# Single banks for all large products, the keys' columns as a pair, and branch sums loaded by the Pool queue, in a fused decoder layer

## The chip, the cores and the metric

The kernel runs on one core of a Trainium2 chip. The metric is the time of one execution on the device in microseconds (us). A core has five engines that run side by side and wait for each other on semaphores: TensorE (PE, matrix products out of SBUF into PSUM), VectorE (DVE), ScalarE (ACT), GpSimd (POOL) and SyncE (SP). DMA transfers are issued here from SP's queue and from POOL's. PSUM has eight banks of 128 x 512 fp32 values. Each engine takes its instructions strictly in the order written for it: an instruction that waits holds up all behind it on that engine or queue.

## The reference, cut to what matters

One layer of a hybrid decoder, for 512 prompt tokens and 8 x 4 sample tokens (T = 544 rows of x together), model width 2048:

```
u = x @ w_in            # split by columns: q_m k_m v_m o_m z_m (2048 each), q_a (2048),
                        # k_a v_a (256 each), z_a g_m g_a (2048 each), i f (4 each)
h_m = mLSTM(q_m, k_m, v_m, ig, log_sigmoid(f), state C, n, m)      # 4 heads of 512
h_a = sliding window attention(q_a, k_a, v_a, 128 wide, ALiBi, sinks)   # 32 heads of 64, 4 kv heads
br_m = headnorm(h_m) * sigmoid(o_m) * silu(z_m);   br_a = h_a * silu(z_a)
y   = sigmoid(g_m) * (br_m @ w_proj_m) + sigmoid(g_a) * (br_a @ w_proj_a)
out = layernorm(alpha * x + y @ w_out)
# also put out: new C, n, m, and key/value buffers of the window:
k_buf_sample = concat(state_attn_k, k_a)[:, 4:];   v_buf_sample likewise
```

The sample rows attend to the window in `state_attn_k` and `state_attn_v`, and 124 of the 128 rows of each new buffer are copies of the old one. All is fp32.

## The kernel before, in words

**Products.** x is kept transposed, as 16 blocks k of [128, 544]. Every fp32 operand of a large product is split in a high part (an ACT cast to fp32r, `wh`, L196; for activations L236) and a low part (a DVE subtraction, `wl`, L197, or L237), and a product is hi·hi + hi·lo + lo·hi: three matmuls. There are two forms.

- `gemm` (L215): 128 output columns, 16 k x 3 x 2 halves of 272 rows = 96 matmuls of 128 x 272 (L205) into one "mm" tile of two PSUM banks. It is used for the columns of V and K of the attention, for all of w_proj_a, for columns 0 to 2 and 13 to 15 (of 16 blocks) of w_proj_m, and for w_out. `tick()` between k runs one step of the side work that is waiting.
- `paired` (L632): two blocks of 128 columns by a scheme of Strassen's kind: seven half products n = 0 to 6 of 24 matmuls each (`half_product`, L599 and L601), 168 in place of 192. It needs sums of the quarters of x (`s1`, `n2`, `n3`, `s4`; the list `XS`) and of the quarters of the weights, made in `prepare` (L572): t1 = b11 + b12, b11 = t1 + b22, b12 += b22, b21 += b11, by DVE adds (L579). Where a pair has `acc`, the last two go as accumulating DMA transfers of POOL's queue (L577). `gather` (L603) collects the products out of three single banks into two tiles. Weights for two products ahead are prepared at high priority.

Raw weights are loaded by SP into three buffers `raw` (b11, b12) and three `raw2` (b22, b21); there are two buffers each of `wh` and `wl`. A load waits on SP's queue until its buffer has been read for the last time.

**PSUM.** Four banks hold small results ("sm"). The other four are opened by `open_psum`: as two "mm" tiles of two banks for gemms, or as four "bank" tiles for pairs; it is called at each change of form.

**Stages.** 0 to 89 us: x comes in 16 loads of 128 x 512 and 4 of samples, is transposed on PE, four transposes to a PSUM tile, and split; two gemms for V, with the gates' products (L340) between their halves; two gemms for K. Beside them `x_sums` (L482) makes s1, n2 and n3 from the split parts, on DVE and in eight operations on POOL (L487, L491); `last_sum` makes s4 beside the first pair. After the K gemms, in SP's queue from 27 us, stand the copies of the old key and value states to their outputs (L541, L542, 992 KB each). 89 to about 1810 us: 72 pairs of columns of w_in, the first 35 with `acc`; the first ones are gates' and mLSTM columns as filling, then 16 pairs of q_a and z_a, each followed by a step of attention (`attentions`, L779; the keys of a kv head come back from scratch memory in `kv_head`, L679, L680, and are cast on ACT). To about 2120 us: 16 gemms of w_proj_a, with the prompt's mLSTM beside them. 2130 to 2320 us, the merge: three gemms of w_proj_m, five pairs, three gemms. Beside the first three `operand_sums` loads the branch br_m from scratch memory (L1406, on SP, four steps of two loads of 544 KB into two buffers) and makes the four sums that the pairs need; the pairs here have no `acc`. Then w_out and the layer norm, to the end.

**Order.** Instructions are put in each engine's order by a planner that works on the program with priorities: `tc.high_priority(offset=...)` moves what stands in it ahead by so much, and `tc.issue_after(x)` keeps DMA issues behind x. `spawn` and `tick` feed side work in small steps (each `yield` ends one).

Of the kernel before, what the change touches and what calls it, by code (L numbers as in the profile page):

```python
# [20 lines left out]
D = 2048  # L21
# [52 lines left out]
def _build(tc, nc, i, o, es):  # L74
# [111 lines left out]

    def load_half(wv, c0, half):
        raw = wr.tile([128, 8, 128], F32, tag="raw", name=nm("raw"))
        state["load"] = nc.sync.dma_start(raw[:], wv[:, half * 8:half * 8 + 8, c0:c0 + 128])
        return raw  # L190

    def split(raw, p=None, tags=("wh", "wl")):
# [3 lines left out]
        A.copy(wh[:], raw[:])  # L196
        V.tensor_tensor(out=wl[:], in0=raw[:], in1=r32(wh[:]), op=ALU.subtract)  # L197
        return wh, wl

    def products(ps, half, wh, wl, xh, xl, cols, every=8):  # L200
        for kk in range(8):
            k = half * 8 + kk
            for n, (a, b) in enumerate(((wh, xh), (wh, xl), (wl, xh))):
                for f, c, w in cols:
                    PE.matmul(ps[:, f, :w], a[:, kk], b(k, c, w),  # L205
                              start=(k == 0 and n == 0), stop=(k == 15 and n == 2))
# [4 lines left out]

    def mm():
        return psA["mm"].tile([128, 2, 512], F32, tag="mm", name=nm("mm"))

    def gemm(wv, c0, xh, xl, cols=EVEN, raws=(None, None), every=8, prio=0, before=None):  # L215
        ps = mm()
        for half in range(2):
# [3 lines left out]
            if prio:  # L221
                with tc.high_priority(offset=prio):
                    wh, wl = split(raw)
            else:
                wh, wl = split(raw)
# [3 lines left out]
    def pv(ps, r=ALL):  # L229
        return ps[r, :, :272]  # L230

    def psamp(ps, r=ALL):
        return ps[r, 1, 240:272]
# [32 lines left out]
    s1, n2, n3 = quad(act2, "s1"), quad(act2, "n2"), quad(act2, "n3")  # L266
# [3 lines left out]
    esG = ExitStack()  # L270
    t544 = pool(esG, "t544", 12)
    tx = pool(esG, "tx", 4)
# [4 lines left out]
    pxs = sm()  # L277
    raw0 = []
    xs_src = i["x_sample"].rearrange("b t d -> (b t) d")
    warm = sm()  # L280
    for _ in range(24):
        PE.transpose(warm[:, 0:128], ident, ident)
    for g in range(4):
        xt = []
        for t in range(4):
            x_ = t5(n=512)
            nc.sync.dma_start(x_[:], i["x_prompt"][0, t * 128:t * 128 + 128, g * 512:g * 512 + 512])
            xt.append(x_)
        xs = ev(512)
        nc.sync.dma_start(xs[:NS], xs_src[:, g * 512:g * 512 + 512])  # L290
        if g < 3:
# [1380 lines left out]
```

## Time and profile before

| | us |
|---|---|
| median of 3 runs | 2543.43 |
| lowest, highest | 2541.89, 2546.58 |
| profiled execution | 2540.61 |
| its span | 2538.8 |

| engine | busy us | share of the span |
|---|---|---|
| PE | 2506.1 | 99% |
| weight loads of PE | 2444.8 | 96% |
| DVE | 1774.0 | 70% |
| ACT | 1208.0 | 48% |
| POOL | 368.9 | 15% |

The granted clock of PE was 0.994 of full speed over the span. Rows of the profile read: start in us, duration in us, engine, line of the kernel, operation, what it writes, what it reads, and in square brackets how long the engine stood idle just before it and what released it. Names have their buffer numbers left out. An engine's busy time is no measure of what it costs; where PE stands idle, the releaser tells who was late.

### The profile page before, as it was taken

To read this page: it belongs to the slowest core of one execution; us is meant where nothing else is said; L and a number is where in the kernel's file an instruction comes from. 1 tells how busy PE (TensorE), PEld (TensorE's weight loads), DVE (VectorE), ACT (ScalarE), POOL (GpSimd) and SP (SyncE) were. 2 spreads that over 40 slices of the span, in tenths; PEclk is the share of its full clock that TensorE was granted. 3 is DMA by queue.
4 is the path that set the end of the run, shared out by engine and by line. 5 is a ranking of instruction groups with operands and counts; after the bars stand their busy time and mean duration, and the time that the engine had idled before them with its cause. 6 is when DMAs were issued, how large, how long until landed. Compare 5 with 4: busy or idle time off the path is not lost.

```text
span 2538.8 us, 48796 instructions
## 1 busy us (share of the span) xinstructions
PE 2506.1 (99%) x19874; PEld 2444.8 (96%) x19874; DVE 1774.0 (70%) x2595; ACT 1208.0 (48%) x1952; POOL 368.9 (15%) x339
## 2 busy tenths in 40 slices
PE   8999999999999999999999999999999999999997
PEld 7999999999999999999999999999999999999997
DVE  7867677777677777687777878777755654874236
ACT  4457676676676665433433434444633332433221
POOL 2111211211211211221111222211000000000002
PEclk9999999999999999999999999999999999999999
DMA  6576666666666654467576576575755556558432
GB/s 193 132 174 163 149 149 164 147 150 164 150 146 164 153 149 115 121 214 238 164 229 214 167 218 205 164 233 179 232 183 173 180 177 194 155 176 264 110 96 84
DMA packets 543026, 433.58 MB, mean 171 GB/s; under 512 B 44080, under 2 KB 449888, under 8 KB 542512
## 3 DMA queue, kind: packets, MB, share of 16 engines
q1 hardware_dynamic: 532720, 393.74, 51.7%
q0 software_dynamic: 10080, 36.70, 7.9%
q8 instruction: 156, 2.56, 0.4%
q14 instruction: 70, 0.57, 0.1%
HBM read 305.74 MB, written 90.04 MB: 156 GB/s over the span
## 4 chain that ended last, share of the span: by engine, by line
PE 91%; DVE 2%; DMA 1%; issue 1%; ACT 1%; SPq 0%; DVEq 0%; ACTq 0%
PE bank L599 41%; PE bank L601 20%; PE mm L205 16%; PE sm L1264 2%; PE sm L1084 1%; PE sm L1078 1%; PE sm L1296 1%; PE sm L705 1%; PE sm L1309 1%; PE sm L743 1%; PE sm L733 1%; PE sm L205 1%; DVE wl L197 1%; ACT wh L196 1%; DMA raw<-in_w_in 0%
## 5 line engine op out<-in xcount | busy, mean ns | idle before, releaser
L196 ACT CAST wh<-raw 128x1024 fp32r<-128x1024 f32 x619 | 648.2, 1047 | 876.5 <-PE bank L599 616.4
L197 DVE TENSOR_TENSOR wl<-raw,wh 128x1024 fp32r<-128x1024 f32 x619 | 763.9, 1235 | 300.7 <-ACT wh L196 266.0
L599 PE MATMUL bank<-xk,wh 128*128 128x272 f32 x2304 | 317.4, 288 | 0.0
L579 DVE TENSOR_TENSOR raw<-raw,raw 128x1024 f32<-128x1024 f32 x238 | 303.0, 1276 | 7.5 <-DMA raw<-in_w_in 3.3
L599 PEld LDWEIGHTS bank<-xk,wh 128*128 128x128 f32 x2304 | 299.8, 188 | 3.4 <-ACT wh L196 1.7
L618 POOL TENSOR_TENSOR ev<-p,ev 128x272 f32<-128x272 f32 x77 | 116.2, 1509 | 680.9 <-ACT ev L617 623.7
L601 PE MATMUL bank<-xk,wl 128*128 128x272 f32 x1152 | 171.0, 288 | 0.0
L599 PE MATMUL bank<-s4h,wh 128*128 128x272 f32 x616 | 159.5, 290 | 0.6
L599 PE MATMUL bank<-n3l,wh 128*128 128x272 f32 x616 | 159.5, 290 | 0.0
L599 PE MATMUL bank<-s1h,wh 128*128 128x272 f32 x616 | 159.3, 290 | 0.0
L599 PE MATMUL bank<-n3h,wh 128*128 128x272 f32 x616 | 159.1, 289 | 0.0
L599 PE MATMUL bank<-n2l,wh 128*128 128x272 f32 x616 | 158.6, 289 | 0.0
L599 PE MATMUL bank<-n2h,wh 128*128 128x272 f32 x616 | 158.6, 288 | 0.0
L599 PE MATMUL bank<-s1l,wh 128*128 128x272 f32 x616 | 158.6, 290 | 0.0
L599 PE MATMUL bank<-s4l,wh 128*128 128x272 f32 x616 | 158.3, 290 | 0.0
L601 PEld LDWEIGHTS bank<-xk,wl 128*128 128x128 f32 x1152 | 154.6, 188 | 0.0
L205 PE MATMUL mm<-bh,wl 128*128 128x272 f32 x704 | 148.3, 290 | 2.2 <-DVE wl L197 2.2
L599 PE MATMUL bank<-a11h,wh 128*128 128x272 f32 x576 | 149.0, 290 | 0.5 <-ACT wh L196 0.5
L599 PE MATMUL bank<-a11l,wh 128*128 128x272 f32 x576 | 148.8, 291 | 0.0
L205 PE MATMUL mm<-bh,wh 128*128 128x272 f32 x704 | 147.9, 291 | 0.6 <-DVE ev L628 0.6
L205 PE MATMUL mm<-bl,wh 128*128 128x272 f32 x704 | 147.9, 289 | 0.0
L599 PEld LDWEIGHTS bank<-s4h,wh 128*128 128x128 f32 x616 | 115.8, 188 | 2.1 <-ACT wh L196 1.7
(439 smaller groups left out, 5719.2 us busy)
## 6 DMA issues: line engine op xcount, KB each, us to landing
raw<-in_w_in SPq DMA_DIRECT2D x296, 512.0 KB
raw<-raw POOLq DMA_DIRECT2D x70, 512.0 KB, 5.0
C<-in_state_mlstm_C SPq DMA_DIRECT2D x32, 1024.0 KB
out<-C SPq DMA_DIRECT2D x64, 512.0 KB
raw<-in_w_proj_a SPq DMA_DIRECT2D x32, 512.0 KB
raw<-in_w_proj_m SPq DMA_DIRECT2D x32, 512.0 KB
raw<-in_w_out SPq DMA_DIRECT2D x32, 512.0 KB
d_sgm<-ev SPq DMA_DIRECT2D x16, 272.0 KB
```

The costliest lines, as they stand in the source:

```text
L196: A.copy(wh[:], raw[:])
L197: V.tensor_tensor(out=wl[:], in0=raw[:], in1=r32(wh[:]), op=ALU.subtract)
L205: PE.matmul(ps[:, f, :w], a[:, kk], b(k, c, w), start=(k == 0 and n == 0), stop=(k == 15 and n == 2))
L579: V.tensor_tensor(out=w[out][:], in0=w[a][:], in1=w[b][:], op=ALU.add)
L599: PE.matmul(ps, wh[:, k], x(p, k), start=(first and k == 0 and p == 0), stop=False, skip_group_check=True)
L601: state["end"] = PE.matmul(ps, wl[:, k], x(0, k), start=False, stop=(k == 7), skip_group_check=True)
L618: G.tensor_tensor(out=c22, in0=p1, in1=c11, op=ALU.subtract)
L705: PE.matmul(pp[:, c0 + w0:c0 + 256], qs[a][:, j * 128:j * 128 + 128], kx[:, k0:k0 + 256 - w0], start=(n == 0), stop=(n == 1))
L733: PE.transpose(pt[:, (m - m0_) * 128:(m - m0_) * 128 + 128], s_[:, b, 128:256] if own else s_[:, b + 1, 0:128], ident)
L743: PE.matmul(po[:, b * 128:b * 128 + n], VA[:, b], p_[:, 2 * b:2 * b + n // 128], start=(b == 0 and m == 0), stop=(b == 3 and m == 1), skip ...
L1078: PE.matmul(pC[c * 32:c * 32 + 32, :], qz[:, c], ct[:, c], start=(b == 0), stop=(b == NB - 1), tile_position=(0, c * 32))
L1264: PE.matmul(pp[:, 0:258], a[:, b * 128:b * 128 + 128], b_[:, b, f], start=(b == 0 and n == 0), stop=(b == 3 and n == 2))
```

## The change

- PSUM: `open_psum` is gone. Four single banks serve both forms. A gemm takes two of them, and what evacuates it is two operations of 272 in place of one of 544 (`halves`).
- Start: x comes in six loads of 128 x 4 x 256 or 512, the samples in two; the order of loads is x, weights, x, samples, x, weights, and so on; 20 instead of 24 warm-up transposes. The raw sums of x are made on DVE from the transposes' PSUM tiles and the parts just split (`s1r`, `n2r`, `n3r`); POOL has none of them. `x_sums` then finishes n2, splits the three, and after V makes s4 in place. Constants and biases are loaded after x. The priority in this stage is 500 where it was 150.
- Keys: the two gemms of K become one pair, the first of the work list, with `acc`; there are 73 pairs in that list now. `attn_values` and `attn_keys` begin some ticks later, and the gates' chain is cut in more steps.
- The copies of the states, 2 x 992 KB, and of the new rows to them, move from the end of the K gemms to the opening of `attentions`. The negation of the sinks moves there too.
- Merge: the five pairs of w_proj_m have `acc`; `operand_sums` has eight steps of one k pair, each with one load of [128, 2, 544] by POOL's queue, and the sums and splits are 272 wide, 64 operations of DVE for 32. The priority of the six gemms' splits is 400 where it was 150.

The core of the diff:

```diff
-    esP, psA = es.enter_context(ExitStack()), {}
-
-    def open_psum(pairs):
-
-        esP.close()
-        psA["mm"] = pool(esP, "psP" if pairs else "psA", 4 if pairs else 2, PSUM)
-
-    open_psum(False)
+    psA = pool(es, "psA", 4, PSUM)
...
+    def bank():
+        return psA.tile([128, 512], F32, tag="bank", name=nm("bank"))
+
     def mm():
-        return psA["mm"].tile([128, 2, 512], F32, tag="mm", name=nm("mm"))
...
+        return [bank(), bank()]
...
+    for _ in range(20):
+        PE.transpose(warm[:, 0:128], ident, ident)
+    raw0, xt, xs = [], [], []
+    for c0, n in ((0, 256), (256, 256), (512, 512), (1024, 512), (1536, 256), (1792, 256)):
+        t_ = xr.tile([128, 4, n], F32, tag=f"x{n}", name=nm("xr"))
+        xdma = nc.sync.dma_start(t_[:], xp_src[:, :, c0:c0 + n])
+        xt += [t_[:, :, c:c + 128] for c in range(0, n, 128)]
+        if c0 == 0:
+            raw0.append(load_half(win, VA_, 0))
...
             else:
-                hilo(pt[:], xk2[0][g - 2][:, q, 0:SEQ], xk2[1][g - 2][:, q, 0:SEQ])
...
+                hilo(pt[:], xk2[0][k // 4 - 2][:, k % 4, 0:SEQ], xk2[1][k // 4 - 2][:, k % 4, 0:SEQ])
+                c = (slice(None), k - 8, slice(0, SEQ - HT))
+                V.tensor_tensor(out=s1r[c], in0=pt[:, HT:SEQ], in1=s1r[c], op=ALU.subtract)
...
+                for ch in (g - 1, g):
+                    ks_ = two_k(ch)
+                    V.tensor_tensor(out=s1r[:, ks_], in0=r32(a21[0][:, ks_]), in1=r32(a21[1][:, ks_]), op=ALU.add)
...
+        if g == 3:
+            for ch in range(4):
+                ks_ = two_k(ch)
+                V.tensor_tensor(out=n2r[:, ks_], in0=r32(a11[0][:, ks_]), in1=r32(a11[1][:, ks_]), op=ALU.add)
+                V.scalar_tensor_tensor(n3r[:, ks_], n2r[:, ks_], -1.0, s1r[:, ks_], op0=ALU.mult, op1=ALU.subtract)
...
     def x_sums():
-
         for ch in range(4):
...
-            G.tensor_tensor(out=r21[:], in0=r32(a21[0][:, ks_]), in1=r32(a21[1][:, ks_]), op=ALU.add)
...
-            G.tensor_tensor(out=r11[:], in0=r32(a11[0][:, ks_]), in1=r32(a11[1][:, ks_]), op=ALU.add)
...
     def ahead_of_sums():
-        return tc.high_priority(offset=150)
+        return tc.high_priority(offset=500)
...
-    for kk in range(2):
-        ps = gemm(win, KA + kk * 128, xh, xl, every=4, prio=150)
-        kt = ev()
-        with ahead_of_sums():
-            A.copy(two(kt[:]), pv(ps))
-            attn_keys(kk, kt)
-    drain()
-    for src, dst in ((d_ks, kb_s), (d_vr[SEQ:T], vb_s)):
-        nc.sync.dma_start(dst[:, 124:128].rearrange("b t k d -> b t (k d)"), src.rearrange("(b t) c -> b t c", t=NTS))
-    nc.sync.dma_start(kb_s[:, 0:124], i["state_attn_k"][:, NTS:128])
-    nc.sync.dma_start(vb_s[:, 0:124], i["state_attn_v"][:, NTS:128])
...
     def attentions():
         while gates_ in live:
             yield
-        for _ in last:
-            pass
         esG.close()
+        with tc.issue_after(state["gates_end"].ins):
+            V.tensor_scalar(nsinkb[:], sinkb[:], -1.0, None, op0=ALU.mult)
+        with tc.issue_after(state["load"].ins):
+            for src, dst in ((d_ks, kb_s), (d_vr[SEQ:T], vb_s)):
+                nc.sync.dma_start(dst[:, 124:128].rearrange("b t k d -> b t (k d)"),
+                                  src.rearrange("(b t) c -> b t c", t=NTS))
+            nc.sync.dma_start(kb_s[:, 0:124], i["state_attn_k"][:, NTS:128])
+            nc.sync.dma_start(vb_s[:, 0:124], i["state_attn_v"][:, NTS:128])
...
+    def end_keys(o1, o2):
+        for kk, o_ in enumerate((o1, o2)):
+            spawn(attn_keys(kk, o_))
...
-    work = [fill.pop(0) for _ in range(3)]
+    work = [pair(KA, KA + 128, end_keys)] + [fill.pop(0) for _ in range(3)]
...
-        for ch in range(4):
-            two_ = []
-            for k in (2 * ch, 2 * ch + 8):
-                t_ = tx.tile([128, 2, T], F32, tag="tx", name=nm("tx"))
-                nc.sync.dma_start(t_[:], src[k:k + 2].rearrange("k p t -> p k t"))
-                two_ += [t_[:, :, 0:HT], t_[:, :, HT:T]]
-            r11, r21, r12, r22 = two_
-            ks_ = slice(ch * 2, ch * 2 + 2)
+        for k in range(8):
+            t_ = tx.tile([128, 2, T], F32, tag="tx", name=nm("tx"))
+            G.dma_start(out=t_[:], in_=src[k:k + 9:8].rearrange("k p t -> p k t"))
+            r11, r21, r12, r22 = (t_[:, a, c:c + HT] for a in range(2) for c in (0, HT))
...
-        sg = merge(pv(gemm(wm, ct * 128, bmh, bml, every=4, prio=150)))
+        sg = merge([p_[:, :HT] for p_ in gemm(wm, ct * 128, bmh, bml, every=4, prio=AHEAD)])
...
-    paired([dict(wv=wm, x=XM, cA=ct * 128, cB=ct * 128 + 128, scale=1.0, end=end_merge(ct)) for ct in range(3, 13, 2)])
+    paired([dict(wv=wm, x=XM, cA=ct * 128, cB=ct * 128 + 128, scale=1.0, acc=True, end=end_merge(ct)) for ct in range(3, 13, 2)])
```

More of the change, by code (lines that the diff above doesn't have):

```diff
@@ L195, in split @@
         wl = p.tile([128, 8, 128], F32R, tag=tags[1], name=nm("wl"))
-        A.copy(wh[:], raw[:])
-        V.tensor_tensor(out=wl[:], in0=raw[:], in1=r32(wh[:]), op=ALU.subtract)
+        n = 8 // parts
+        for k in range(0, 8, n):
+            A.copy(wh[:, k:k + n], raw[:, k:k + n])
+            V.tensor_tensor(out=wl[:, k:k + n], in0=raw[:, k:k + n], in1=r32(wh[:, k:k + n]), op=ALU.subtract)
         return wh, wl
@@ L1384, in _build @@
         ps = gemm(wa_, ct * 128, bah, bal, every=2)
[L1385 removed]
+        for p_, s_ in halves(ps, sg):
+            V.tensor_tensor(out=s_, in0=p_, in1=s_, op=ALU.mult)
         nc.sync.dma_start(d_t[ct], sg[:])
```

227 lines of the change are left out of this document (125 added, 102 removed).

## The prediction

> **What bounds the kernel now.** I read the page first, then the busy time in stretches of 20 us, then TensorE's own timeline at each stretch that is not full, and from there the engine named as releaser.
>
> ```profile
> span 2538.8 us, 48796 instructions
> PE 2506.1 (99%) x19874; PEld 2444.8 (96%) x19874; DVE 1774.0 (70%) x2595; ACT 1208.0 (48%) x1952; POOL 368.9 (15%) x339
> PE 91%; DVE 2%; DMA 1%; issue 1%; ACT 1%; SPq 0%; DVEq 0%; ACTq 0%
> ```
>
> PE (TensorE) is busy 99% of the span and carries 91% of the chain that ended last. So there are two ways to win: fewer matmuls, or closing the few holes. The stretches say where the holes are (columns: stretch, its length, busy PE, weight load, DVE, ACT, POOL each with its count, granted clock, DMA share, GB/s):
>
> ```profile
> 0.00:20.00 20.00, 13.51 (x74) 11.88 (x75) 6.57 (x14) 6.47 (x14) 2.96 (x7) 0.83 0.88 255
> 20.00:40.00 20.00, 19.67 (x158) 18.55 (x157) 16.43 (x30) 10.92 (x28) 6.45 (x5) 1.00 0.68 201
> 40.00:60.00 20.00, 16.33 (x117) 15.83 (x117) 19.74 (x27) 10.51 (x19) 8.17 (x8) 0.91 0.54 146
> 120.00:140.00 20.00, 19.41 (x151) 18.64 (x151) 11.87 (x20) 8.16 (x13) 2.72 (x3) 1.00 0.68 152
> 140.00:160.00 20.00, 20.00 (x162) 20.00 (x161) 12.61 (x15) 10.27 (x14) 3.17 (x3) 1.00 0.86 214
> 2160.00:2180.00 20.00, 16.90 (x121) 16.49 (x120) 17.21 (x22) 6.90 (x10) 0.00 (x0) 0.91 0.59 193
> 2260.00:2280.00 20.00, 19.03 (x151) 18.62 (x150) 15.77 (x19) 8.20 (x10) 1.44 (x1) 1.00 0.46 137
> 2280.00:2300.00 20.00, 19.38 (x155) 19.19 (x154) 14.63 (x21) 9.34 (x13) 0.00 (x0) 1.00 0.98 313
> ```
>
> A full stretch holds 162 matmuls, 0.123 us each. Counting what is missing against 162 at 0.125 us: 40 to 60 us lacks 45 (5.6 us), 120 to 140 lacks 11 (1.4), 2160 to 2180 lacks 41 (5.1), the two around 2280 lack 11 and 7 (2.3). The first 20 us are filling. In 40 to 60 us DVE (VectorE) is busy 19.74 of 20: that stretch is DVE's, not PE's. The holes themselves:
>
> ```profile
> 43.01 1.11 PE L460 MATMUL sm<-cc,ev 128*128 128x128 f32 x4 [2.39 <-ACT ev L530]
> 44.81 0.43 PE L205 MATMUL mm<-a21l,wh 128*128 128x272 f32 x1
> 45.04 0.43 PE L205 MATMUL mm<-a11h,wl 128*128 128x272 f32 x1
> 46.77 0.29 PE L205 MATMUL mm<-a21h,wh 128*128 128x272 f32 x1
> 46.89 0.29 PE L205 MATMUL mm<-a11l,wh 128*128 128x272 f32 x1
> 57.11 0.52 PE L205 MATMUL mm<-xk,wl 128*128 128x272 f32 x2 [1.28 <-DVE wl L197]
> 89.06 0.33 PE L473 MATMUL sm<-cc,ev 128*128 128x128 f32 x1 [1.44 <-ACT ev L536]
> 89.26 0.37 PE L599 MATMUL bank<-a11h,wh 128*128 128x272 f32 x1
> 2165.09 0.52 PE L205 MATMUL mm<-bh,wl 128*128 128x272 f32 x2 [2.19 <-DVE wl L197]
> ```
>
> After the 2.39 us hole matmuls start 0.23 us apart (44.81, 45.04) until about 46.4, then 0.12 (46.77, 46.89): a hole of 2 us and more costs some 1.7 us again in slow matmuls. [...]
>
> **The change, part by part.**
>
> *Keys as a pair.* Two gemms of 96 matmuls become seven half products of 24: 168 instead of 192. 24 x 0.125 = 3.0 us off PE, in a place where nothing else can fill it. The pair needs the sums of x that the gemms did not, and so brings DVE's work on them forward by 26 us. That is the price, next.
>
> *Sums of x, start.* DVE's rows around the second V column block, whose low part PE waits for:
>
> ```profile
> 11.65 1.23 DVE L197 TENSOR_TENSOR wl<-raw,wh 128x1024 fp32r<-128x1024 f32 x1 [8.92 <-ACT wh L196]
> 28.87 0.68 DVE L237 TENSOR_TENSOR xk<-sm,xk 128x512 fp32r<-128x512 f32 x1
> 29.47 1.28 DVE L492 TENSOR_TENSOR tx<-tx,tx 128x544 f32<-128x544 f32 x1
> 41.68 1.22 DVE L197 TENSOR_TENSOR wl<-raw,wh 128x1024 fp32r<-128x1024 f32 x1
> 42.82 0.72 DVE L237 TENSOR_TENSOR s1l<-tx,s1h 128x544 fp32r<-128x544 f32 x1
> 43.45 0.72 DVE L237 TENSOR_TENSOR n3l<-tx,n3h 128x544 fp32r<-128x544 f32 x1
> 55.84 1.21 DVE L197 TENSOR_TENSOR wl<-raw,wh 128x1024 fp32r<-128x1024 f32 x1
> ```
>
> From start to start a 512-wide operation takes 0.60 us (28.87 to 29.47), a 1024-wide one 1.14, a 544-wide one 0.63; by width a 272-wide one comes to about 0.36 and a 240-wide one to 0.33 (estimates from these). In the changed kernel's instruction order DVE does ahead of that low part, that included: 3 of 1024, 22 of 544, 7 of 512, 8 of 272, 15 of 240 and 6 small ones of 0.2: 3.4 + 14.0 + 4.2 + 2.8 + 4.9 + 1.5 = 30.8 us. Before, the like count is 22.1 us, stretched by POOL at work beside it (the 1.28 for a 0.7 operation at 29.47) and by some 6 us of waiting for x. DVE began at 11.65 and was done at 42.9. After, POOL has no more sums, x comes in six larger loads, and DVE can start near 9.7 (the first weights' landing): 9.7 + 30.8 + about 2 of waiting = 42.5. So the first V hole barely moves: DVE trades idle time and contention for eight more microseconds of its own work. The wait at 43.01 on the copy of V vanishes (the transposes now come some ticks later), but the low part takes its place 0.4 us earlier.
>
> The second low part stood at 55.84 to 57.05. After, 4.2 us of last sums and low parts of x, 0.3 of gates, 5.1 of s4, 1.1 of a pair's add and its own 1.1 follow 43.3: 55.7. PE: 48 matmuls more, 61.7; the low parts of s4 and of the first pair are queued behind, 4 x 0.63 + 1.14, and I add 1.8 us for them: the first half product at 63.5. The pair takes 168 x 0.125 = 21.0 and the transposes of keys 0.5: 85.0 against 89.26. **−4.2 us** for start and keys, 3.0 of it the matmuls. Bounds: −2 if DVE waits longer for x than 2 us, −11 if none of the holes at 43, 57 and 89 nor the filling is left (9.2 us of holes and slow clock, less what the filling must keep, with the 3.0). I take −4.2 because DVE's own count bounds it. The gates' chain is cut into more steps (about 11 more turns); nobody waits for it until the first attention, some 50 us later, so I cost it at nothing. The four warm-up transposes fewer stand before the first x has landed: nothing. Sinks' negation and constants later: nothing, same cover.
>
> *State copies and the keys' way to the attention.* The two 992 KB copies of the states move on SP's queue from 27 us to the opening of the attentions, right ahead of further weights and of the loads of keys from scratch memory.
>
> ```profile
> 27.10 0.79 SPq L541 DMA_DIRECT2D out<-in_state_attn_k  x1
> 34.94 5.30 SPq L189 DMA_DIRECT2D raw<-in_w_in  x1
> 127.32 1.42 SPq L679 DMA_DIRECT2D s<-d_ka  x2
> 127.61 1.05 ACT L196 CAST wh<-raw 128x1024 fp32r<-128x1024 f32 x1 [2.41 <-PE bank L599]
> 133.14 0.62 ACT L236 CAST k<-s 128x512 fp32r<-128x512 f32 x1 [4.48 <-DMA s<-d_ka]
> 133.97 1.04 ACT L196 CAST wh<-raw 128x1024 fp32r<-128x1024 f32 x1
> ```
>
> Before, the keys' load lands 5.8 us after issue (127.32 to 133.14), ACT stands 4.48 us, and the next weights' cast behind it (133.97) comes a little late: the 1.4 us of 120 to 140. After, the order on SP is: state copies, the next pair's weights, among them one whose buffer is freed only by the low part of the sixth product of the running pair, then the keys. ACT's cast of k stands between the weights' casts of products six and seven. Counted from the start of the fourth product (3 us each), PE bears a landing at +6.75; the buffer frees near +1 to +3, and with 1.8 us of issuing ahead and 5.8 of landing it comes at +8.6 to +10.6. That makes 1.9 to 3.9 us of hole, with slow matmuls 2.9 to 5.6, less the 1.4 there was: **+2.8 us**. Bounds: −1.4 if it is in time, +8 if the 2 MB of copies add to it the 5.3 us that the row at 34.94 shows for a load behind them. I take the middle, as the copies are issued some products earlier.
>
> *Merge.* Two things change by rows of the merge: four DVE adds a pair become two DMA accumulations on POOL's queue and two DVE adds; and the branch comes in eight loads of 544 KB on POOL's queue, one k pair each, instead of eight on SP's in four steps of two.
>
> ```profile
> 2136.36 0.43 SPq L1406 DMA_DIRECT2D tx<-d_brm  x1
> 2142.94 0.72 DVE L1410 TENSOR_TENSOR tx<-tx,tx 128x544 f32<-128x544 f32 x1 [2.51 <-DMA tx<-d_brm]
> 2155.79 9.65 SPq L189 DMA_DIRECT2D raw<-in_w_proj_m  x2
> 2157.52 0.72 DVE L1410 TENSOR_TENSOR tx<-tx,tx 128x544 f32<-128x544 f32 x1 [5.02 <-DMA tx<-d_brm]
> 2163.82 1.22 DVE L197 TENSOR_TENSOR wl<-raw,wh 128x1024 fp32r<-128x1024 f32 x1
> L577 POOL DMA_DIRECT2D raw<-raw x70: 848/860/1058, 79.9 to 896.6; - x70
> raw<-raw POOLq DMA_DIRECT2D x70, 512.0 KB, 5.0
> ```
>
> The 2.19 us hole comes from DVE: it stood 5.02 us for tx, then had six operations of a 544-wide step, an add and the previous block's merge ahead of the low part at 2163.82. Gone are 10 adds of 1.14 (11.4 us); 64 operations of 0.36 replace 32 of 0.63 (+2.9), and 16 merges in halves add 0.1 each (+1.4): some 7 us less on DVE. Stretches 2160 to 2180 and around 2280 lack 5.1 + 2.3 = 7.4 us together. What decides is L, the time from a load's issue to its landing, since DVE, in order, has a step's sums ahead of later low parts. Between freeing a buffer and using it again DVE has about 13 operations, 6.5 us, and the low parts behind have 1 to 1.5 us in hand: L up to about 8 us costs nothing. My L: 0.86 of issuing (row L577) + 6.6 (2136.36 to 2142.94, the same bytes from the same place) = 7.4. Ends: 0.86 + 5.0, the median of the accumulating transfers, = 5.9; and 12.4, if two loads run one after the other (6.6 + 5.8). I take 7.4, the row with the same source. The last load stands on POOL behind the first pair's accumulation and so behind its weights; I leave 2.4 us of loss for it and for the new accumulations, whose cover is that each has two products (6 us) until its cast against 0.86 + 5.0. **−5.0 us**; ends −7.4 and, by L of 12.4, far above zero (rival three). [...]
>
> *Single banks for the gemms.* One 544-wide evacuation becomes two of 272: 16 x 0.1 us on DVE in the stage of w_proj_a, where PE is full and DVE half idle: nothing. Rotation of banks: gates and V hold two each, so the first pair's banks are those of gates and V, both evacuated before V's end: nothing, or the 1.8 above.
>
> Sum: −4.2 + 2.8 − 5.0 = −6.4. The profiled execution took 2540.6 us (span 2538.8), so 2534.2; the median of the runs shown is 2543.4, 2.8 above it, so 2537.0.
>
> **The rivals.**
>
> *One: the start is not DVE's.* If DVE's sums go in parallel with the waits for x and overlap better than my count, the holes at 43, 57 and 89 go with the keys' 3.0: −11, and with the rest −13: 2530. For it: 6 us of DVE idle before 28 us. Against: 30.8 us of work fit nowhere else.
>
> *Two: little is left.* Keys late by +8 and the merge at −2: −4.2 + 6 − 2 = −0.2 to −2: 2542. For it: 9.65 us that SP stood once two loads blocked it; against: weights are loaded two products ahead.
>
> *Three, slower: branch loads on POOL land late.* Two buffers, and steps in pairs: three refills in a row plus the last load are serial, so each microsecond of L beyond 8 costs about 4. At L of 9.6 the whole change comes to zero, at 10.9 to +5.1; at 11.0 the merge loses 2.4 + 12 = 14.4 instead of 7.4: −1.4 + 7.0 = +5.6, 2549, and at 12.4 some 2554. For it: the DVE rows already wait 2.51 and 5.02 us for such loads. Against: both landed in 6.4 to 6.6.
>
> **How the numbers follow.** A measurement here tells 0.2%, 5.1 us, from no change. My forecast has 0.50, of which 0.38 is beyond 5.1 us and 0.12 within; rival one 0.20, all faster; rival two 0.12, within; rival three 0.18, slower. Faster 0.58, same 0.24, slower 0.18. The forecast's own range, from −2 − 1 − 3 less the bounded wait up to −4.2 − 1.4 − 7.4, is 2530 to 2543; with rival one's better end and the start of rival three: 2526 to 2551.
>
> **What the profile after would show.** The first half product on the keys near 63 us, and 24 + 4 fewer matmuls; holes at 43 (on DVE's low part now) of about 2 us, none on the copies of V or K; ACT waiting on the keys' load near 135 us with a PE hole of 2 to 4 us; 10 more accumulations on POOL; no hole above 1 us at 2160; branch loads landing in 6 to 7 us. Wrong would be: the first half product after 66 or before 61; DVE idle over 4 us before 43; no wait on the keys; DVE waiting over 3 us for branch loads in the merge.

## The result and the profile after

The changed kernel took 2531.2 us (median of 6 runs, 2528.2 to 2533.7) against 2540.3 for the one before on the same chip: a ratio of 0.9961, with a 95% interval of 0.9945 to 0.9977. That is 9.2 us less; 6.4 were forecast. A second set of runs gave 0.9960 (0.9946 to 0.9975). The time lies in the range given, but four of the forecast's terms were off, and their errors cancelled in part.

The page of the changed kernel, its first part and its chain:

```profile
span 2531.2 us, 48857 instructions
PE 2501.8 (99%) x19846; PEld 2442.5 (96%) x19846; DVE 1767.3 (70%) x2666; ACT 1214.0 (48%) x1976; POOL 375.7 (15%) x352
PE 91%; issue 4%; DVE 3%; DMA 1%; ACT 0%; POOL 0%; SPq 0%; DVEq 0%; POOLq 0%; ACTq 0%
```

28 matmuls fewer, as 24 and 4 make, and the span is 7.6 us shorter than in the profile before. Its stretches (same columns as before):

```profile
0.00:20.00 20.00, 14.35 (x97) 13.68 (x98) 9.52 (x22) 8.18 (x20) 0.31 (x5) 0.91 0.97 287
20.00:40.00 20.00, 15.15 (x115) 13.75 (x115) 20.00 (x43) 11.90 (x28) 1.85 (x2) 1.00 0.51 104
40.00:60.00 20.00, 18.77 (x147) 18.05 (x146) 19.04 (x31) 9.93 (x22) 2.85 (x3) 1.00 0.50 113
100.00:120.00 20.00, 18.81 (x148) 18.37 (x147) 16.20 (x28) 11.60 (x17) 3.10 (x3) 1.00 0.77 182
120.00:140.00 20.00, 20.00 (x162) 19.81 (x161) 10.64 (x17) 8.32 (x11) 1.53 (x2) 1.00 0.83 254
2160.00:2180.00 20.00, 19.33 (x154) 19.11 (x154) 17.03 (x31) 8.82 (x15) 3.81 (x4) 1.00 0.64 178
2260.00:2280.00 20.00, 20.00 (x162) 20.00 (x161) 11.60 (x16) 6.04 (x8) 2.26 (x2) 1.00 0.72 201
```

40 to 60 us has 147 matmuls instead of 117, the merge's stretch 154 instead of 121, and 2260 to 2280 is full. But 20 to 40 us fell from 158 to 115, with DVE busy 20.00 of 20: DVE does set the pace of the start, only the hole is earlier than I put it, in the low parts of x itself. And 100 to 120 us now lacks 14.

TensorE's holes in the changed kernel:

```profile
10.52 0.68 PE L315 MATMUL sm<-cc,xs 32*128 32x32 f32 x8 [3.00 <-DMA xs<-in_x_sample]
23.45 0.40 PE L204 MATMUL bank<-a11l,wh 128*128 128x272 f32 x1 [1.19 <-DVE a11l L238]
27.32 0.66 PE L311 MATMUL sm<-cc,xr 128*128 128x128 f32 x4 [1.07 <-DVE a21l L238]
43.71 0.39 PE L204 MATMUL bank<-a11h,wh 128*128 128x272 f32 x1 [0.51 <-ACT ev L579]
55.38 0.52 PE L204 MATMUL bank<-xk,wl 128*128 128x272 f32 x2 [0.32 <-DVE wl L196]
60.97 0.29 PE L640 MATMUL bank<-a11h,wh 128*128 128x272 f32 x1
104.51 2.27 PE L640 MATMUL bank<-xk,wh 128*128 128x272 f32 x16 [0.46 <-DVE ev L665]
109.53 0.39 PE L640 MATMUL bank<-s1h,wh 128*128 128x272 f32 x1 [0.73 <-ACT wh L195]
2174.45 0.39 PE L640 MATMUL bank<-n2h,wh 128*128 128x272 f32 x1 [0.67 <-ACT wh L195]
```

The pairs begin with the keys' at 60.97 us. To compare kernels past the shifts I cut every profile at the same instructions: the first matmul of the first half product, of pairs 0, 3, 36, 42 and 71 counted behind the keys (pair 0 is the first of the old list), of the merge's first pair, and the last half product. All numbers are us, worked out from the start times of TensorE's rows; the second rows of a kernel are a second profile of it.

```
kernel            pair 0 at  0 to 3   3 to 36  36 to 42  42 to 71  71 to merge  merge pairs
before               89.26    67.38    778.85    157.06    694.77       385.99       108.30
  again (b0)         90.08    67.92    778.83    162.75    694.77       383.74       108.33
changed              82.95    68.10    778.82    163.31    694.77       380.77       105.97
  again (a0)         82.14    68.89    779.11    162.20    694.77       380.77       106.66
a1_keys_gemm         87.82    63.40    781.13    157.03    694.77       380.77       106.81
a2_merge_noacc       84.53    69.55    779.38    163.75    694.77       380.77       105.16
a3_merge_sp          83.21    68.31    779.43    162.34    694.77       381.96       106.98
b1_merge_before      82.72    69.08    778.82    165.91    694.77       382.90       109.48
b2_copies_early      85.17    68.92    778.82    165.47    694.77       380.77       106.78
b3_x_on_act          81.50    68.65    778.82    162.79    694.77       380.77       106.63
c1_best              81.42    68.10    778.82    157.41    694.77       380.77       105.16
c2_coarse_pool       85.57    69.77    778.82    158.33    694.77       380.77       109.52
c3_copies_last       83.89    68.88    778.82    160.06    694.77       383.04       106.40
d1_load_twice        84.07    68.17    778.82    162.54    694.77       381.99       123.50
```

By this cut (means of two profiles each) the change gains 7.1 us up to pair 0, gives 0.8 back up to pair 3, gains 6.1 from pair 71 to the last half product, and 1.0 behind it, in the last gemms (242.4 us from there to the last matmul, then 241.3). The start varies by itself: the eight profiles of kernels with the changed start and the pair (all but the two of before, a1, b2, b3 and c1) have pair 0 at 82.1 to 85.6 and pair 36, the sum of the first three columns, at 929.9 to 934.2. A difference of one or two us between two profiles means nothing there. The stage from 36 to 42 stands apart: below.

### The profile page after: what moved, and what is told of

It reads as the page before. It is cut to its first block, busy times and chain, and to the rows that moved or that the text cites. A ratio compares the mean times of both kernels' runs of the same rounds, so it can differ in the third digit from the quotient of the medians.

```text
span 2531.2 us, 48857 instructions
## 1 busy us (share of the span) xinstructions
PE 2501.8 (99%) x19846; PEld 2442.5 (96%) x19846; DVE 1767.3 (70%) x2666; ACT 1214.0 (48%) x1976; POOL 375.7 (15%) x352
## 3 DMA queue, kind: packets, MB, share of 16 engines
q1 hardware_dynamic: 531312, 389.29, 51.5%
## 4 chain that ended last, share of the span: by engine, by line
PE 91%; issue 4%; DVE 3%; DMA 1%; ACT 0%; POOL 0%; SPq 0%; DVEq 0%; POOLq 0%; ACTq 0%
PE bank L640 43%; PE bank L642 21%; PE bank L204 13%; PE sm L1312 2%; PE sm L1131 1%; PE sm L1125 1%; PE sm L1344 1%; PE sm L746 1%; PE sm L1357 1%; PE sm L784 1%; PE sm L774 1%; PE sm L204 1%; DMA tx<-d_brm 1%; DMA raw<-in_w_in 0%; DVE z L1614 0%
## 5 line engine op out<-in xcount | busy, mean ns | idle before, releaser
L620 DVE TENSOR_TENSOR raw<-raw,raw 128x1024 f32<-128x1024 f32 x230 | 291.8, 1270 | 8.1 <-DMA raw<-in_w_in 4.5
L640 PE MATMUL bank<-n2l,wh 128*128 128x272 f32 x624 | 162.2, 292 | 0.0
L204 PE MATMUL bank<-bh,wl 128*128 128x272 f32 x704 | 148.3, 289 | 0.0
L204 PE MATMUL bank<-bh,wh 128*128 128x272 f32 x704 | 147.9, 290 | 0.0
L204 PE MATMUL bank<-bl,wh 128*128 128x272 f32 x704 | 147.4, 289 | 0.0
L640 PEld LDWEIGHTS bank<-n2h,wh 128*128 128x128 f32 x624 | 118.5, 190 | 2.0 <-ACT wh L195 0.9
```

The lines of the kernel that those rows point to most:

```text
L204: PE.matmul(ps[f][:, :w], a[:, kk], b(k, c, w), start=(k == 0 and n == 0), stop=(k == 15 and n == 2))
L620: V.tensor_tensor(out=w[out][:], in0=w[a][:], in1=w[b][:], op=ALU.add)
L640: PE.matmul(ps, wh[:, k], x(p, k), start=(first and k == 0 and p == 0), stop=False, skip_group_check=True)
```

## The experiments

**Is the slow stage of the changed kernel its own?** In the first two profiles the sample heads' stage, with the same instructions in the same order, took 6 us more in the changed kernel. Two runs without any edit, of the changed kernel and of the one before:

> The changed kernel again, for a second profile and a narrower interval. In its first profile the time from the first half product of the 39th pair to that of the 41st was 66.5 us against 60.7 before, with no idle TensorE and a granted clock of 0.66 to 0.84 for 40 us. Theory A (a chance dip of the clock, nothing of the change): this time lies between 60 and 62 in this profile, and the span some 5 us below 2531. Theory B (the changed kernel's own alignment of work there): again 66 us and a span of 2531. Ratio to before: 0.994 to 0.998.

> The kernel before again, for a second profile of it. In the stage from the 37th to the 43rd pair of the list after the keys, with the same instructions in the same order, its first profile took 157.0 us; the changed kernel 162.2 and 163.3, with a lower granted clock and no idle TensorE. [...] Theory B (chance from execution to execution): anything from 157 to 164.

The changed kernel again took 162.2 us there, which spoke for theory B of the first; the kernel before, profiled again, took 162.75 where it had taken 157.06. So it is chance from execution to execution (a0's theory A with the wrong number, b0's theory B): over all fourteen profiles the stage takes 157.0 to 165.9, and both a1 and c1, whose code there is the changed kernel's, have 157. The stretches of 10 us of the kernel before, first and second profile:

```profile
1010.00:1020.00 10.00, 10.00 (x75) 9.37 (x73) 4.32 (x5) 3.77 (x7) 3.09 (x4) 0.88 0.23 73
1020.00:1030.00 10.00, 10.00 (x83) 9.25 (x82) 3.64 (x6) 2.98 (x5) 0.00 (x0) 1.00 0.38 105
```

```profile
1010.00:1020.00 10.00, 10.00 (x62) 9.50 (x60) 1.78 (x3) 3.55 (x7) 1.35 (x1) 0.71 0.28 83
1020.00:1030.00 10.00, 10.00 (x61) 9.13 (x61) 3.45 (x4) 1.94 (x5) 1.75 (x3) 0.66 0.19 52
```

TensorE is busy all the time, but the granted clock is 0.71 and 0.66 instead of 0.88 and 1.00. So two spans alone do not tell 5 us of a change from this stage; the cut does.

**Keys as gemms.** Undoes the pair alone:

```diff
+    for kk in range(2):
+        ps = gemm(win, KA + kk * 128, xh, xl, every=4, prio=500)
+        kt = ev()
+        with ahead_of_sums():
+            for p_, k_ in halves(ps, kt):
+                A.copy(k_, p_)
+        spawn(attn_keys(kk, kt))
     state["plain_done"] = True
-    work = [pair(KA, KA + 128, end_keys)] + [fill.pop(0) for _ in range(3)]
+    work = [fill.pop(0) for _ in range(3)]
```

> The changed kernel with the keys' columns as two gemms again, ahead of the pairs. Theory (24 matmuls of 0.125 us, nothing else): the first pair of the work list starts 3.0 us later than in the changed kernel, where it started at 82.95 us, so at about 86, and the whole is 3 us slower, +0.12%. Rival (the matmuls saved are given back, because the sums of x are then not ready for a pair that comes early): same start within 1 us. If more than +5 us the pair also hid the evacuation and transposes of the keys.

Pair 0 came at 87.8, 5 us later, but pairs 0 to 3 took 63.4 instead of 68.1 us and 3 to 36 2.3 more. Of the 23 small matmuls of side work that stand in pairs 0 to 3 of the changed kernel, the 19 of the gates have moved behind pair 3 (2.0 of these 2.3), and the 2.5 us that the products lose there to waits are gone. At pair 36 a1 is at 932.4 us, the changed kernel at 929.9 and 930.1, which would make the pair worth 2.4; but the mean of the eight profiles above is 931.5, and a1 lies inside their range. So the 24 matmuls fewer are certain, and what they are worth in time is not shown. In the median a1 (2529.5 us, ratio 0.9956, 0.9940 to 0.9972) is not to be told from the changed kernel (0.9960).

**The merge, part by part.** Accumulations off; the branch loads on SP's queue; both and the old four steps; and the four steps with POOL's queue:

```diff
 # a2
-    paired([dict(..., scale=1.0, acc=True, end=end_merge(ct)) for ct in range(3, 13, 2)])
+    paired([dict(..., scale=1.0, end=end_merge(ct)) for ct in range(3, 13, 2)])
 # a3
-            G.dma_start(out=t_[:], in_=src[k:k + 9:8].rearrange("k p t -> p k t"))
+            nc.sync.dma_start(out=t_[:], in_=src[k:k + 9:8].rearrange("k p t -> p k t"))
 # b1: operand_sums as in the kernel before, and acc=True away as in a2
 # c2: b1 with
-                nc.sync.dma_start(t_[:], src[k:k + 2].rearrange("k p t -> p k t"))
+                G.dma_start(out=t_[:], in_=src[k:k + 2].rearrange("k p t -> p k t"))
```

> The changed kernel, but the five pairs of the merge add on DVE as before (ten adds of 1.14 us back on DVE). The stretch from 2120 us to the last half product lost 0.9 us of TensorE time in the changed kernel and 7.5 in the one before. Theory A (the adds are the larger part, as 11.4 us of DVE): it loses 4 to 6 us here. Theory B (the holes came from the branch loads and SP's order, not from the adds): it loses 1 to 2.5.

> The changed kernel with the eight branch loads on SP's queue, all else as changed. Theory A (the queue frees the issue order: on SP weights and branch loads block each other, as with 9.65 us before): DVE waits for the branch over 5 us more in sum and TensorE loses 4 to 8 us from 2120 us on, +0.2%. Theory B (all queues feed the same engines and one order serves as well): within 1.5 us of the changed kernel, which lost 0.9.

> The changed kernel with the merge's branch in four steps of two loads on SP and DVE adds in its pairs, as before, but with the priority of 400 and halves. From the 72nd pair to the last half product the kernel before took 494.3 us, the changed one 486.7 and 487.4, without accumulations 485.9, with SP's queue 488.9. Theory A (the fine steps are the gain): 492 to 495 here. Theory B (the priority of the gemms' splits is the gain): 486 to 489.

> The kernel b1_merge_before (branch in four steps of two loads, DVE adds), but its loads on POOL's queue. From the 72nd pair to the last half product b1_merge_before took 492.4 us; fine steps on POOL's queue with DVE adds 485.9. Theory A (fineness is the gain): 491 to 493 here. Theory B (the queue is the gain): 486 to 488. Between them if both.

From pair 71 to the last half product the sums of the last two columns are 486.7 and 487.4 for the changed kernel, 485.9 without accumulations, 488.9 by SP's queue, 492.4 with the old steps on SP, 490.3 with the old steps on POOL, and 494.3 and 492.1 for the kernel before. The whole times go the same way: the ratios to the kernel before are 0.9954 for a2, 0.9966 for a3, 0.9989 (0.9974 to 1.0004) for b1 and 0.9972 for c2. So the fine steps are the larger part: 490.3 to 485.9, 4.4 us from c2 to a2, whose edits differ in nothing else, and all of it in the pairs.

How they do it is open. The last sum of the branch is done at 2180.92 us in c2. By the first matmuls of the pairs, its first pair takes 22.73 us and a2's 21.05, and only there do sums stand on DVE. But the second to fourth pairs take 21.50, 21.50 and 21.46 in c2 and 21.06 each in a2, though neither runs a sum any more, and the rest, 1.3, lies in the fifth (half a microsecond of it four matmuls of the next gemm that moved ahead). That is 2.7 of the 4.4. In these pairs of c2, as in the kernel before and in b1, TensorE begins the product with s4 ahead of the one with n3 and waits at it for a cast that waits for one of the pair's own adds; in a2 n3 comes first, as written, with no wait. From c2:

```profile
2221.80 1.68 DVE L620 TENSOR_TENSOR raw<-raw,raw 128x1024 f32<-128x1024 f32 x1
2223.50 1.05 ACT L195 CAST wh<-raw 128x1024 fp32r<-128x1024 f32 x1 [2.62 <-DVE raw L620]
2224.60 0.19 PEld L640 LDWEIGHTS bank<-s4h,wh 128*128 128x128 f32 x1 [0.36 <-ACT wh L195]
```

So with other steps the planner gave the later pairs another order. No run holds that order fixed, and none parts the size of a step from its buffers either: an old step needs both buffers at once, a fine one only one, so that the next load can run beside it.

In this stretch b1 differs from the kernel before by the priority, the halves and the single banks alone, and its 492.4 is not clear of that kernel's 492.1. c2 lies between its two theories, as it should if both the steps and the queue count. POOL's queue is worth 2.1 us (b1 to c2), all of it ahead of the pairs: in the fine form a3 loses 1.2 us there, where DVE waits longer for its first loads and, at 2161.64, 0.71 us for weights of SP's queue. From the a3 run, DVE's waits and the hole behind them:

```profile
2141.01 0.44 DVE L1454 TENSOR_TENSOR tx<-tx 128x272 f32<-128x272 f32 x1 [5.28 <-DMA tx<-d_brm]
2153.51 0.44 DVE L1454 TENSOR_TENSOR tx<-tx 128x272 f32<-128x272 f32 x1 [3.18 <-DMA tx<-d_brm]
2164.40 0.52 PE L204 MATMUL bank<-bh,wl 128*128 128x272 f32 x2 [0.92 <-DVE wl L196]
```

The accumulations gain nothing: without them the pairs run 0.8 to 1.5 us faster, at 105.2 us with no hole above 0.15 us, though DVE has 11.4 us more. Theory B of a2 was right in kind, but went below its own bound. In a3 DVE waits 5.2 us more for the branch than in the changed kernel (10.4 in sum, 5.2 there), as theory A said, but the whole stretch is only 1.9 us over the changed kernel's mean, between the two bounds and nearer to B: most of DVE's waiting cost TensorE nothing. The page of the changed kernel counts both queues on the same 16 DMA engines, the one of SP's transfers with 51.5% of their span and the one of POOL's with 9.8%. On b1 theory A held.

**Slower loads.** The third rival's price, measured by doubling L:

```diff
+            for _ in range(2):
                 G.dma_start(out=t_[:], in_=src[k:k + 9:8].rearrange("k p t -> p k t"))
```

> The changed kernel, but each branch load of the merge is issued twice into the same tile, the second behind the first's landing, so that L, from issue to the landing that counts, is 2 x (0.73 + 6.2) = 13.9 us where it is 6.9. Theory (the prediction's third rival: L up to 8 us costs nothing, each microsecond more costs about 4 by three serial refills and the last load): from the 72nd pair to the last half product 487 + 4 x 5.9 = 511 us, 505 to 517, and the whole slower than the kernel before by some 14 us, +0.5%. Rival (the loads have more slack than that, since steps can fall into the first pair): under 497 us and no slower than before.

505.5 us, 18.4 more than the changed kernel's mean, and slower than the kernel before: 1.0026 (1.0011 to 1.0041). The mechanism of the rival is there. Its 4 us for each us of L beyond 8 comes out at 3.1 (18.4 over 5.9) if L was the 13.9 that was planned. The rows have less: in the five steps that DVE waited for, the time from the first issue to DVE's start was 11.1 to 14.2 us, 12.9 in the mean, and by that it is 3.8 (18.4 over 4.9). The run's TensorE holes are in the first pair, behind the sums of the last steps:

```profile
2176.55 0.40 PE L640 MATMUL bank<-s1h,wh 128*128 128x272 f32 x1 [2.92 <-ACT wh L195]
2184.61 0.60 PE L640 MATMUL bank<-s1h,wh 128*128 128x272 f32 x1 [3.26 <-ACT s1h L237]
2192.95 0.59 PE L640 MATMUL bank<-s1h,wh 128*128 128x272 f32 x1 [5.85 <-ACT s1h L237]
```

**The copies of the states**, put back early, and put behind all pairs:

```diff
 # both: out of attentions()
-            nc.sync.dma_start(kb_s[:, 0:124], i["state_attn_k"][:, NTS:128])
-            nc.sync.dma_start(vb_s[:, 0:124], i["state_attn_v"][:, NTS:128])
 # b2: ahead of  state["plain_done"] = True ;  c3: behind the drain() after paired(work),
 # there under  with tc.issue_after(state["load"].ins):
```

> The changed kernel with the two 992 KB copies of the states put back in SP's queue behind the V columns. Theory (they are behind no critical transfer where they stand now: the accumulation that took 13.5 us beside them and the keys' load were hidden): pairs 0 to 3 take the 68.1 us of the changed kernel within 1 us, and the whole is the same within 2 us. Rival (the copies delay weights where they stand): pairs 0 to 3 2 us shorter, or the first pair over 2 us later by their traffic in the filling.

> The changed kernel with the two 992 KB copies of the states put behind the last pair, at the begin of the products of w_proj_a. Theory (where they stand in the changed kernel they delay nothing on the path; the hole of 0.5 and the 0.7 us near 104 and 109 us are the gates' chain): the first half product as in the changed kernel, pairs 0 to 3 within 68.1 to 69.5 us. Rival of the prediction (they stand in the way of weights and keys): pairs 0 to 3 at 66.5 or less, the accumulation's 13.5 us back to under 7.

In b2 the planner put the copies at 6.55 us, between the loads of x, much earlier than the 27 us of the kernel before. Pair 0 came at 85.2, but the eight kernels that have the changed kernel's start spread over 82.1 to 85.6 themselves: inconclusive on the start. Pairs 0 to 3 took 68.9 in both, inside 68.1 to 69.8 of the others: where they stand in the changed kernel the copies delay nothing on the path, although they do delay a transfer. In c3 they cost something where they went: the column from pair 71 to the merge has 383.04 instead of 380.77, with a TensorE hole of 2.04 us at 1800.64, and the whole ratio is 0.9967 (b2: 0.9976). The accumulating transfers' time from issue to landing, of the changed kernel and of c3:

```profile
DMA to landing us min/median/max: 4.5/4.9/13.5
```

```profile
DMA to landing us min/median/max: 4.5/4.9/6.8
```

**DVE's part of the start.** The raw quarters of x come from ACT:

```diff
+                A.copy(n2r[:, k], pt[:, 0:HT])
+                A.copy(s1r[:, k, 0:SEQ - HT], pt[:, HT:SEQ])
...
-                for ch in (g - 1, g):
-                    ks_ = two_k(ch)
-                    V.tensor_tensor(out=s1r[:, ks_], in0=r32(a21[0][:, ks_]), in1=r32(a21[1][:, ks_]), op=ALU.add)
+                A.copy(s1r[:, k4, SEQ - HT:HT], src)
...
-                V.tensor_tensor(out=n2r[:, ks_], in0=r32(a11[0][:, ks_]), in1=r32(a11[1][:, ks_]), op=ALU.add)
```

> The changed kernel, but the raw quarters of x that the sums begin with are copied out of PSUM by ACT (16 copies of 272 or 240 and 2 small ones, some 6.5 us of ACT) in place of eight 544-wide DVE additions (5.1 us). From 20 to 40 us DVE was busy 20.00 of 20 us and TensorE lost 6.4 us. Theory (DVE sets the pace of the start): the first half product, at 60.97 and 59.96 us in the changed kernel, comes 2 to 4 us earlier. Rival (ACT, 60% busy there and ahead of each DVE split, takes its place): same or up to 3 us later.

The first half product came at 59.86 us. The kernels with the changed start have 59.96 to 63.75, so that is a gain of 0.1 to 3.9, not the clear 2 to 4: DVE gave up 5.1 us and was still busy all of 20 to 40 us. Ratio 0.9961 (0.9946 to 0.9976), the changed kernel's own.

**Three edits together.** b3, a2, and `if k == 1:` before the samples' transposes made `if k == 3:`

> Three edits on the changed kernel: raw quarters of x copied by ACT as in b3_x_on_act, no accumulations in the merge as in a2_merge_noacc, and the 16 transposes of the samples put behind the fourth instead of the second block of x, since TensorE stood 3.0 us for the samples' load at 7.5 us. Theory (the filling waits for what is asked too early, and accumulations bring the merge nothing): first half product 2 to 3 us before the 59.9 of b3_x_on_act, merge at 485.9 us from the 72nd pair on, the whole 3 us under the changed kernel: ratio to before 0.995. Rival (the samples' wait only covers another wait for x or DVE): first half product within 1 us, ratio 0.996.

The first half product came at 59.12, 0.7 us before b3's, which is within the spread of the start: the samples' wait had covered another. The hole at the start is now 2.00 us for x itself:

```profile
10.87 1.10 PE L311 MATMUL sm<-cc,xr 128*128 128x128 f32 x8 [2.00 <-DMA xr<-in_x_prompt]
41.80 0.40 PE L204 MATMUL bank<-a11h,wh 128*128 128x272 f32 x1 [0.51 <-ACT ev L578]
53.49 0.52 PE L204 MATMUL bank<-xk,wl 128*128 128x272 f32 x2 [0.32 <-DVE wl L196]
```

The merge took its 485.9. The whole took 2526.2 us, ratio 0.9941 (0.9924 to 0.9957) to the kernel before: the best of this study. Its interval still touches the changed kernel's (0.9946 to 0.9975), and against that kernel directly it was not timed.

## Why the prediction was right, and where not

- *Keys as a pair, −3.0.* The matmuls are gone; the time is not shown. At pair 36 a1 is 2.4 us behind the changed kernel, but only 0.9 behind the mean of the eight profiles, and these spread over 4 us.
- *Start, −1.2 beside the keys.* Too small. The eight profiles with this start have pair 0 at 83.6 us in the mean, 6.0 before the 89.7 of the two before, where keys and start together were put at 4.2. The first low part of the second V columns was forecast done at 42.5, the second at 55.7, the first half product at 63.5; the changed kernel's first profile has 41.8, 55.3 and 60.97:

```profile
8.23 1.23 DVE L196 TENSOR_TENSOR wl<-raw,wh 128x1024 fp32r<-128x1024 f32 x1 [5.43 <-ACT wh L195]
40.57 1.22 DVE L196 TENSOR_TENSOR wl<-raw,wh 128x1024 fp32r<-128x1024 f32 x1
54.10 1.23 DVE L196 TENSOR_TENSOR wl<-raw,wh 128x1024 fp32r<-128x1024 f32 x1 [0.88 <-PE bank L204]
57.79 1.22 DVE L196 TENSOR_TENSOR wl<-raw,wh 128x1024 fp32r<-128x1024 f32 x1
```

  DVE began at 8.23 instead of 9.7 and had 2.5 us of waiting where 2 were put; its count of 30.8 us held (the parts listed make 30.5). The mis-sized term is the 1.8 us that I added for low parts queued ahead of the first pair: its own came at 57.79, three us before it was asked for. The sum for the second low part was also miscounted: 43.3 and the five terms behind it make 55.1, not 55.7. Which part of the new start brings the gain is open: loads, priority, single banks and the sums taken off POOL changed together, and no run takes one of them back alone. a1, without the pair, is at pair 36 already 3.8 us ahead of the two profiles before (932.4 against 935.5 and 936.8).
- *Slow matmuls behind a hole of 2 us and more.* Not a rule. In the second profile of the kernel before, the holes of 2.38 us at 43.83 and 2.46 at 57.93 were followed by matmuls at the full granted clock of 1.00, and so was the 2.04 in c3; of the five holes of 2.0 to 2.5 us behind the filling, the two of the first profile of the kernel before alone had slow ones behind them. Part of the 5.6 and 5.1 us that the forecast counted as missing there was chance.
- *Gates' chain at nothing.* Wrong by 1.4 to 2.5 us: its small operations on DVE now stand among the low parts of the first pairs, and 100 to 120 us lacks 14 and 21 matmuls in the two profiles, where the kernel before lacked 3 and 1, by the holes at 104.51 on a gathering operation of DVE (L665) and at 109.53.

```profile
99.88 1.28 DVE L438 TENSOR_TENSOR_SCAN t<-t,t 4x544 f32<-4x544 f32 x1
102.90 1.21 DVE L196 TENSOR_TENSOR wl<-raw,wh 128x1024 fp32r<-128x1024 f32 x1
104.04 0.42 DVE L665 SCALAR_TENSOR_TENSOR ev<-bank,ev 128x272 f32<-128x272 f32 x1
```

  The cover I named (nobody waits for the gates) was right; that others wait behind them in DVE's order was left out. It is the case of what is queued behind, not of who waits for it. (The reading is from the rows; no run took the chain away. In a1, where the chain's matmuls come behind pair 3, pairs 0 to 3 have no hole.)
- *Keys' way to the attention, +2.8.* This step failed. No hole came: 120 to 140 us is full, and the 11 matmuls that it lacked before (18 in the second profile) are back, 1.4 and 2.2 us, which is the lower bound of this step and not its middle. With the gates' chain the net is a loss of 1.2 us: pairs 0 to 3 take 68.8 in the mean of the eight, 67.7 before.

```profile
123.59 0.68 SPq L831 DMA_DIRECT2D out<-in_state_attn_v  x1
129.47 0.48 SPq L611 DMA_DIRECT2D raw<-in_w_in  x1
139.02 1.23 SPq L720 DMA_DIRECT2D s<-d_ka  x2
```

```profile
138.89 1.05 ACT L195 CAST wh<-raw 128x1024 fp32r<-128x1024 f32 x1 [4.60 <-DMA raw<-raw]
143.45 0.62 ACT L237 CAST k<-s 128x512 fp32r<-128x512 f32 x1 [1.19 <-DMA s<-d_ka]
146.22 2.09 ACT L195 CAST wh<-raw 128x1024 fp32r<-128x1024 f32 x2
```

  The weights' load that I had the keys stand behind went out at 129.47, a good product earlier than the low part I took to release its buffer; the keys' load then waited until 139.02 for the gates' transposes on TensorE, which I had not seen, and landed 4.4 us after its issue, not 5.8. The fourth product began at 138.91, so the landing was at +4.5 where +8.6 to +10.6 was forecast and +6.75 was the limit. The copies stood in the way of an accumulation (the 4.60), with no cost. ACT's order shows in its wait for the keys: for 1.19 us it did nothing until they landed, and evacuated the fourth product only behind their cast, at 143.97, though its last matmul had ended at 142.18.
- *Merge, −5.0.* Gained 7.1, with the 1.0 of the last gemms, where 7.4 was the end of the range. L was 0.73 + 6.2 = 6.9 against my 7.4. The loads landed in 5.0, 6.2 and 9.1 us (least, median, most), and DVE's waits for them are 0.42, 1.44, 0.57 and 2.78 us:

```profile
2141.34 0.44 DVE L1454 TENSOR_TENSOR tx<-tx 128x272 f32<-128x272 f32 x1 [0.42 <-DMA tx<-d_brm]
2151.19 0.44 DVE L1454 TENSOR_TENSOR tx<-tx 128x272 f32<-128x272 f32 x1 [1.44 <-DMA tx<-d_brm]
2156.17 0.44 DVE L1454 TENSOR_TENSOR tx<-tx 128x272 f32<-128x272 f32 x1 [0.57 <-DMA tx<-d_brm]
2171.02 0.44 DVE L1454 TENSOR_TENSOR tx<-tx 128x272 f32<-128x272 f32 x1 [2.78 <-DMA tx<-d_brm]
DMA to landing us min/median/max: 5.0/6.2/9.1
```

  The reason was only half right. I counted the adds taken from DVE as the main relief; a2 shows that they bring nothing, and c2 against a2 that the finer steps, which I had as a cost of 2.9 us on DVE, bring 4.4. So DVE's sum of work was the wrong measure. In its place the runs show waits that depend on the order: 1.7 us in the first pair, where the sums stand among the low parts, and 2.7 in pairs where none stands. The 2.4 us that I left for the last load and the accumulations were 0.8 to 1.5, all in the first pair: the last load, issued at 2163.20 with an accumulation issued at 2160.74, reached DVE 7.8 us later; in a2, without accumulations, it took 5.9. The move to POOL's queue brought 2.1 us (b1 to c2), all ahead of the pairs, where 382.90 became 380.77, and nothing in the pairs (109.48 and 109.52).
- *Rivals.* One (all start holes go) did not come: 20 to 40 us has more of them. Two did not come (its sum took 6 us for the 8 that it names for the keys; with 8 it is +1.8). Three is a real mechanism, 18 us when each load was issued twice, and did not come because L stayed at 6.9.
- *Signs of being wrong.* One showed: the first half product came before 61, at 60.97 and 59.96. Another can be read both ways: DVE's longest wait for a branch load was 2.78 us, under the 3, but its waits add up to 5.2. ACT did wait for the keys, 1.19 us, with no hole on TensorE.

In sum the forecast had two gains too small (start by 1.8, merge by 2.1) and a cost too large (keys' load and gates' chain together: 2.8 forecast, 1.2 measured): 5.5 us too little by the cut, −11.9 for −6.4. The stage between pairs 36 and 42 took 2.8 us of it back in the two profiles' means, by chance. The medians show 9.2, with 5.8 to 14 by the interval. So the direction and the two stages that gain were understood; that the sum came out this near is partly luck, since the largest cost in it did not exist and the merge gained for another reason.

## What to carry to other kernels

When side work shares an engine with what the critical engine waits for, its sum of busy time says little: eight short steps took away what ten adds fewer did not. Then look where the gain falls before naming its cause: here more than half of it fell in pairs in which no step runs any more, and which the planner had put in another order. A cost put at nothing because nobody waits for its result still has to be checked for who stands behind it in the same queue. And compare two profiles between the same instructions, stage by stage, before reading a difference of some microseconds in the span: one stage here differs by 9 us between executions of the same code.

## What was not expected of the hardware

A stage that keeps TensorE busy can lose its clock. The samples' heads send runs of 32 small matmuls (128 x 32 and 32 x 32) between full products. In the changed kernel TensorE is busy 10.00 of 10 us from 1000 to 1010, at a granted clock of 0.66. In its run from 1000.32 to 1004.71 us two of these matmuls take 0.23 us, and from the middle of the run 0.35, with no idle time (1002.38 to 1002.61 to 1002.96); the full products behind go at 0.23 us each from 1005.85 to 1009.25 instead of 0.125:

```profile
1002.38 0.30 PE L950 MATMUL sm<-PT,vas 32*64 32x32 f32 x2
1002.61 0.42 PE L949 MATMUL sm<-PT,vb 128*64 128x32 f32 x2
1002.96 0.42 PE L950 MATMUL sm<-PT,vas 32*64 32x32 f32 x2
```

The same instructions cost 157.0 to 165.9 us for six pairs. What lowers the clock is not shown: in the first profile of the kernel before, the first such run, from 1005.44 us, keeps to 0.23 us until its last two at 1008.88, and no run here takes the small matmuls away or moves them. The filling, too, varies by itself: the first half product of the same code comes between 59.96 and 63.75 us, with TensorE waiting 0.6 to 4.5 us for the samples' load.
